# Weight sums of a seven-product feed-forward layer: 64 half-partition DMAs, one behind each block product, with two small reorderings

## The chip, the core and the metric

The kernel runs on one core of one Trainium2 chip. The metric is the device time of one launch in microseconds (us). The median of three runs before the change is 1150.55 us (1150.04 to 1153.35). One further launch was profiled; the trace that is quoted here is of that launch. The engines are called as the profile calls them: PE (TensorE matmuls) and PEld (its weight loads), DVE (VectorE), ACT (ScalarE), POOL (GpSimd), SP (SyncE, which here only issues DMAs).

## The reference

One decoder layer on 512 tokens of width 1024, in float32: a SwiGLU feed-forward half step, a token mixer (two kinds of attention), and a second feed-forward half step. "Part one" and "part two" are the two feed-forward steps. The change touches them alone:

```
def swiglu(x, w_gate, w_up, w_down):
    return (jax.nn.silu(x @ w_gate) * (x @ w_up)) @ w_down
h = rms_norm(x, ffn1_pre[l])
x = x + 0.5 * rms_norm(swiglu(h, ffn1_w_gate[l], ffn1_w_up[l], ffn1_w_down[l]), ffn1_post[l])
```

The hidden width is 2816, which is 22 blocks of 128.

## The kernel before

Every float32 matmul is made of three matmuls in a faster 32-bit format: each operand is split into a rounded part `hi` and the rest `lo`, and `hi*hi`, `hi*lo` and `lo*hi` are added up (`mm3`, L148 to L153). The rounded part of a weight tile is made by ACT (L128, tile `whi`), the rest by DVE (L129, tile `wlo`). There are three `whi` and three `wlo` buffers of 128x1024, so DVE and ACT can be at most three weight tiles ahead of PE.

Gate and up products use a scheme with seven block products in place of eight. The hidden blocks go in 11 groups p of two blocks each. Groups 0 and 1 (`PLAIN`) are computed plainly. From group 2 on, each group has seven products P1, P2, P6, P5, P7, P4, P3, with P1 of the next group between P7 and P4. A product is eight weight tiles of 128x128 against 256 token columns, 24 matmuls in all. `prep` makes its weight tile, which for P6, P5 and P3 is a sum or a difference of the four weight blocks of the group (L465: s1 = block + block; L466: s2; L480 and L477: differences made in place). `run` issues the matmuls; `finished` adds the products up: P1, P6 and P7 are copied out of PSUM by ACT into tiles `V_s` (L500), and DVE adds the next product to them (L504 behind P2, L509 behind P7, L516 behind P3). Then `swiglu` follows (L358, L359, L360), and after P3 the sums of the hidden activations (`sums`, L363 to L382), which are stored to DRAM.

Weight blocks come through a ring of three `raw` tiles of two halves each. `refill` (L314) issues the next 512 KB load on SP's queue when a half has been read for the last time. The loads stand in one list: gate and up blocks, then the blocks for the down projection.

The down projection uses the same scheme, so it needs four sums of down weights, T1 to T4. They are formed in DRAM by DMAs from DRAM to DRAM that POOL issues, some with addition (`table_sums`): for each quarter of the hidden groups, two copies, two more copies, two additions of a weight quarter, one addition of one sum to another, one more such addition. In part one this happens while the gate and up products run. The table `SUMS` says which steps follow which group: after a group's activations are there, POOL copies one column of them into a tile `mark` (L389), and the DMAs of that row of the table are issued behind this copy. In part two the sums were formed during the mixer, with the same transfers.

Part one begins in `opening`, where the order on ACT, DVE and PE is the order of the code. It computes the products of group 0 and half of group 1 on unnormalised tokens, the row of inverse norms (`row`), and the sums of tokens T1 to T4 (`scaled_sums`), which the seven products need. Elsewhere the framework's scheduler places the instructions of each engine before the launch; on the chip each engine runs its own list strictly in order.

`ffn_down` runs the products B11, T2, T3, T1, B21, B22, T4. In `product` the weights of the last `tail` hidden groups are held, so that the first 128 tokens are finished ahead of the second; B22 has tail 4, T4 has tail 6.

Of the kernel before, what the change touches and what calls it, by code (L numbers as in the profile page):

```python
# [12 lines left out]
F32 = mybir.dt.float32  # L13
# [4 lines left out]
OP = mybir.AluOpType  # L18
# [12 lines left out]
PLAIN = 2  # L31
AHEAD = 2
# [3 lines left out]
SUMS = [((0, 0),), ((0, 1), (1, 0)), ((0, 2), (1, 1)), ((0, 3), (1, 2)), ((0, 4), (2, 0)), ((1, 3), (2, 1)), ((1, 4), (2, 2)),  # L36
        ((2, 3), (3, 0)), ((2, 4), (3, 1)), ((3, 2),), ((3, 3),), ((3, 4),)]
# [24 lines left out]
class Layer:  # L62
# [257 lines left out]
    def ffn(self, gu, wd, td, post, finish, xsrc, aside=None, opened=None):  # L320
# [5 lines left out]
        later = LATER if opened else NP  # L326

# [34 lines left out]
        def sums(p, ev, od):  # L362

            h = slice(0, 256), slice(256, 512)
            x, y = self.slot("CB" if p < KEEP else "PT"), self.slot("ring")
# [17 lines left out]
        def extra(p):  # L383
            if opened:
                sums_behind((E[p] if p >= later else E[p][0].bitcast(F32))[:, 0:1], p + 1)

        def sums_behind(src, n):
            mark = self.sbt("mark", [P, 1])
            behind = nc.gpsimd.tensor_copy(mark, src).ins  # L389
            with self.tc.issue_after(behind):  # L390
                for g, step in SUMS[n]:
                    self.table_sums(wd, td, 3 * g, step)

        banks = dict(opened["banks"]) if opened else {}
        if opened:
            tops = opened["tops"]
            sums_behind(row[:, 0:1], 0)
# [97 lines left out]
        def finished(p, name):  # L495
            st = state[p]
            t0, t1 = slice(0, 256), slice(256, 512)
            if name in ("P1", "P6", "P7"):
                v = self.slot("V")
                nc.scalar.copy(v, st["X"])  # L500
                st[name + "c"] = v
            if name == "P2":
# [3 lines left out]
                st["od"] = self.slot("W")  # L506
                swiglu(st["ev"][:, t0], v[:, t0], v[:, t1], t0)
# [3 lines left out]
            elif name == "P4":  # L511
                b = st["X"]
                swiglu(st["od"][:, t0], b[:, t0], b[:, t1], t0)
            elif name == "P3":
                v = st["P6c"]
                nc.vector.tensor_add(v, st["Z"], v)  # L516
                swiglu(st["ev"][:, t1], v[:, t0], v[:, t1], t1)
# [14 lines left out]
        self.ffn_down(E, later, kept, wd, td, post, finish, xsrc, aside, opened)  # L532
# [48 lines left out]
    def scaled_sums(self, tags, xt, g, out):  # L581
# [19 lines left out]
        out["T3"] = self.keep_sum(tags, diff(4, hi, lambda j: xt[j][:, hi]))  # L601
        yield
        t1 = less(lambda j: xt[j][:, hi], lambda j: xt[j][:, lo])
        out["T1"] = self.keep_sum(tags, t1)
        yield
        t2 = diff(4, hi, of(t1))
        out["T2"] = self.keep_sum(tags, t2)
# [3 lines left out]
    def ffn_down(self, E, later, kept, wd, td, post, finish, xsrc, aside, opened):  # L611
# [91 lines left out]

        a = [self.bank("F") for _ in range(2)]
# [983 lines left out]
```

## Time and profile before

| what | value |
| --- | --- |
| median of three runs | 1150.55 us |
| the profiled launch, its own time | 1148.57 us |
| its span, from the first to the last instruction | 1146.8 us |
| mean granted TensorE clock | 0.991 |
| PE busy | 1106.8 us (97%) |
| DVE busy | 879.5 us (77%) |
| ACT busy | 638.7 us (56%) |
| POOL busy | 130.7 us (11%) |

The profiled launch took 1.77 us more than its span, the median 1.98 us more than the profiled launch. Opening and the gate and up products of part one fill the first 255 us or so; its down projection ends near 350 us. The gate and up products of part two begin near 800 us, the down projection fills the last 140 us. Times within the profile count from the first instruction. In a row of the timeline stand the start, the duration, the engine, the line, the operation and the tiles, and in brackets how long the engine had been idle and for whom. In a row of windows stand the busy time of each engine with its count of instructions, the granted clock (PEclk), the busy share of the 16 DMA engines and what they moved.

### The profile page before, as it was taken

To read this page: it belongs to the slowest core of one execution; us is meant where nothing else is said; L and a number is where in the kernel's file an instruction comes from. 1 tells how busy PE (TensorE), PEld (TensorE's weight loads), DVE (VectorE), ACT (ScalarE), POOL (GpSimd) and SP (SyncE) were. 2 spreads that over 40 slices of the span, in tenths; PEclk is the share of its full clock that TensorE was granted. 3 is DMA by queue.
4 is the path that set the end of the run, shared out by engine and by line. 5 is a ranking of instruction groups with operands and counts; after the bars stand their busy time and mean duration, and the time that the engine had idled before them with its cause. 6 is when DMAs were issued, how large, how long until landed. Compare 5 with 4: busy or idle time off the path is not lost.

```text
span 1146.8 us, 18400 instructions
## 1 busy us (share of the span) xinstructions
PE 1106.8 (97%) x6863; PEld 979.7 (85%) x6863; DVE 879.5 (77%) x1554; ACT 638.7 (56%) x1151; POOL 130.7 (11%) x186
## 2 busy tenths in 40 slices
PE   9989799999999999999999999999999999999996
PEld 7889799987878977777888898887989999998885
DVE  5978798998668788788545465885788989979574
ACT  7445345466455677687555534554435555548552
POOL 0212101100003025456000000000000000000000
PEclk9989899999999999999999999999999999999999
DMA  9879795679956369996243425475233434369862
GB/s 353 277 237 245 223 274 177 181 216 290 306 184 184 97 193 299 293 278 139 84 129 120 131 66 136 147 245 180 83 107 129 151 121 130 121 208 324 274 188 88
DMA packets 106569, 218.08 MB, mean 190 GB/s; under 512 B 20432, under 2 KB 50160, under 8 KB 106480
## 3 DMA queue, kind: packets, MB, share of 16 engines
q1 hardware_dynamic: 97120, 170.51, 45.6%
q0 software_dynamic: 9216, 46.14, 15.8%
q8 instruction: 54, 0.88, 0.3%
q10 hardware_dynamic: 144, 0.26, 0.1%
q14 instruction: 35, 0.29, 0.1%
HBM read 195.60 MB, written 67.42 MB: 229 GB/s over the span
## 4 chain that ended last, share of the span: by engine, by line
PE 59%; DVE 21%; DMA 10%; issue 4%; ACT 4%; POOL 2%; DVEq 0%; POOLq 0%; SPq 0%; ACTq 0%
PE pb_F L153 8%; PE pb_F L151 8%; PE pb_F L152 8%; DVE wlo L129 7%; PE pb_S L153 5%; PE pb_S L151 5%; PE pb_S L152 5%; DMA raw<-in_gu_dram 4%; PE pb_T L152 4%; PE pb_T L153 4%; PE pb_T L151 4%; PE pb_V L151 2%; PE pb_V L152 2%; PE pb_V L153 2%; DMA tmp_t<-in_x_dram 1%
## 5 line engine op out<-in xcount | busy, mean ns | idle before, releaser
L129 DVE TENSOR_TENSOR wlo<-raw,whi 128x1024 fp32r<-128x1024 f32 (+2 forms) x237 | 280.4, 1185 | 120.0 <-ACT whi L128 115.9
L128 ACT CAST whi<-raw 128x1024 fp32r<-128x1024 f32 (+2 forms) x237 | 241.8, 1021 | 204.6 <-PE pb_F L152 53.2
L151 PE MATMUL pb_F<-xhl_t,whi 128*128 128x512 f32 (+1 forms) x440 | 155.1, 352 | 1.7 <-DVE Q_s L1328 1.0
L153 PE MATMUL pb_F<-xhl_t,wlo 128*128 128x512 f32 (+1 forms) x440 | 154.3, 351 | 1.1 <-DVE wlo L129 1.0
L152 PE MATMUL pb_F<-xhl_t,whi 128*128 128x512 f32 (+1 forms) x440 | 153.7, 349 | 0.0
L153 PE MATMUL pb_S<-xhl_t,wlo 128*128 128x256 f32 (+1 forms) x280 | 86.0, 308 | 13.0 <-DVE wlo L129 13.0
L153 PEld LDWEIGHTS pb_F<-xhl_t,wlo 128*128 128x128 f32 x440 | 82.7, 188 | 12.0 <-DVE wlo L129 2.4
L151 PEld LDWEIGHTS pb_F<-xhl_t,whi 128*128 128x128 f32 x440 | 82.8, 188 | 11.7 <-DVE Q_s L1328 1.2
L152 PEld LDWEIGHTS pb_F<-xhl_t,whi 128*128 128x128 f32 x440 | 82.8, 188 | 9.7 <-issue 0.2
L151 PE MATMUL pb_S<-xhl_t,whi 128*128 128x256 f32 (+1 forms) x280 | 85.5, 305 | 0.1
L152 PE MATMUL pb_S<-xhl_t,whi 128*128 128x256 f32 (+1 forms) x280 | 85.1, 304 | 0.0
L172 POOL TENSOR_TENSOR rs_t<-rs_t,mhalf_t 128x1 f32<-128x1 f32 x20 | 13.0, 649 | 598.4 <-DVE rs_t L168 598.4
L153 PEld LDWEIGHTS pb_S<-xhl_t,wlo 128*128 128x128 f32 x280 | 54.7, 195 | 16.4 <-DVE wlo L129 14.2
L1077 POOL TENSOR_SCALAR SP_s<-SP_s,st_t 128x384 f32<-128x384 f32 (+2 forms) x48 | 51.7, 1129 | 71.6 <-DVE st_t L1013 61.5
L151 PEld LDWEIGHTS pb_S<-xhl_t,whi 128*128 128x128 f32 x280 | 54.6, 195 | 2.7 <-DVE V_s L509 0.3
L152 PEld LDWEIGHTS pb_S<-xhl_t,whi 128*128 128x128 f32 x280 | 54.6, 195 | 2.2
L153 PE MATMUL pb_T<-xhl_t,wlo 128*128 128x256 f32 x200 | 55.8, 279 | 0.6 <-DVE wlo L129 0.6
L151 PE MATMUL pb_T<-xhl_t,whi 128*128 128x256 f32 x200 | 55.7, 278 | 0.0
L152 PE MATMUL pb_T<-xhl_t,whi 128*128 128x256 f32 x200 | 55.5, 278 | 0.0
L465 DVE TENSOR_TENSOR tmp_t<-raw 128x1024 f32<-128x1024 f32 x18 | 22.0, 1224 | 37.8 <-DMA raw<-in_gu_dram 37.8
L151 PE MATMUL pb_S<-SP_s,whi 128*128 128x256 f32 x160 | 44.6, 279 | 1.2 <-ACT V_s L500 1.2
L128 ACT CAST whi<-tmp_t 128x1024 fp32r<-128x1024 f32 x36 | 37.8, 1051 | 12.8 <-ACT W_s L359 5.0
(837 smaller groups left out, 3236.4 us busy)
## 6 DMA issues: line engine op xcount, KB each, us to landing
raw<-in_gu_dram SPq DMA_DIRECT2D x84, 512.0 KB, 4.4
tdram<-in_d_dram POOLq DMA_DIRECT2D x36, 768.0 KB, 11.2
raw<-tdram SPq DMA_DIRECT2D x40, 512.0 KB, 4.8
raw<-in_w_in_dram SPq DMA_DIRECT2D x18, 1024.0 KB, 5.5
raw<-in_d_dram SPq DMA_DIRECT2D x30, 512.0 KB, 4.4
tdram<-tdram POOLq DMA_DIRECT2D x12, 768.0 KB, 8.7
tdram<-in_d_dram POOLq DMA_DIRECT2D x12, 512.0 KB, 9.8
odram<-W_s SPq DMA_DIRECT2D x22, 256.0 KB, 2.0
```

Of the source, the lines that this page charges most:

```text
L128: self.last_cast = self.nc.scalar.copy(dsthi, src).ins
L129: self.nc.vector.tensor_sub(dstlo, src, dsthi.bitcast(F32))
L151: mm(out, lhi, rhi, start=start, stop=False, skip_group_check=skip)
L152: mm(out, lhi, rlo, start=False, stop=False, skip_group_check=skip)
L153: mm(out, llo, rhi, start=False, stop=stop, skip_group_check=skip)
L172: nc.gpsimd.tensor_tensor(out=r, in0=v, in1=self.mhalf, op=OP.pow)
L465: nc.vector.tensor_add(s1, blk(p, 0, 1), blk(p, 1, 1))
L1077: self.last_pool = nc.gpsimd.tensor_scalar(pp, pp, st[:, 1, t:t + 1], None, op0=OP.mult).ins
```

## The change

Four things are changed.

1. The sums of part one are issued by a generator `sum_steps` in place of `table_sums`. Each transfer is cut into two of 64 partitions, so 32 become 64, in the order of `SUM_STEPS`. Two are issued behind the row of norms, two behind each plain group, and from group 2 on one behind each of six places in `finished`: behind the ACT copies of P1, P6 and P7, behind the DVE additions of P2 and P3, and at P4. The last four follow at the start of `ffn_down`. Each place has its own `mark` copy on POOL. Part two keeps `table_sums` in the mixer.
2. The sums x of the activations of groups 1 and 2 go to slots of the tag `of` in place of the one slot `CB`.
3. In `opening` the token sums are made in another order, and the squares of the tokens stand between them.
4. B22 holds three groups at its end in place of four, in both parts.

```
+SUM_STEPS = [((2, (0, 1), 0), (3, (1, 1), 0)), ((0, (1, 1), 0), (1, (1, 0), 0)), ((2, (0, 0), 1), (3, (0, 1), 1)), ((0, 2, 1),),
+             ((1, 0, 1),)]
-SUMS = [((0, 0),), ((0, 1), (1, 0)), ((0, 2), (1, 1)), ((0, 3), (1, 2)), ((0, 4), (2, 0)), ((1, 3), (2, 1)), ((1, 4), (2, 2)),
-        ((2, 3), (3, 0)), ((2, 4), (3, 1)), ((3, 2),), ((3, 3),), ((3, 4),)]
+X_TAGS = "CB", "of", "of"
...
         def sums(p, ev, od):
-            x, y = self.slot("CB" if p < KEEP else "PT"), self.slot("ring")
+            x, y = self.slot(X_TAGS[p % 3] if p < KEEP else "PT"), self.slot("ring")
...
         def extra(p):
-            if opened:
-                sums_behind((E[p] if p >= later else E[p][0].bitcast(F32))[:, 0:1], p + 1)
+            if p < PLAIN:
+                sums_behind(E[p][0][:, 0:1].bitcast(F32), 2)
 
         def sums_behind(src, n):
-            mark = self.sbt("mark", [P, 1])
-            behind = nc.gpsimd.tensor_copy(mark, src).ins
-            with self.tc.issue_after(behind):
-                for g, step in SUMS[n]:
-                    self.table_sums(wd, td, 3 * g, step)
+            if opened and n:
+                mark = self.sbt("mark", [P, 1])
+                behind = nc.gpsimd.tensor_copy(mark, src).ins
+                with self.tc.issue_after(behind):
+                    for _ in range(n):
+                        next(steps, None)
...
                 nc.scalar.copy(v, st["X"])
                 st[name + "c"] = v
+                sums_behind(v[:, 0:1], 1)
             if name == "P2":
                 v = st["P1c"]
                 nc.vector.tensor_add(v, st["Y"], v)
...
+                sums_behind(v[:, t1][:, 0:1], 1)
...
             elif name == "P4":
+                sums_behind(st["od"][:, t1][:, 0:1], 1)
...
                 nc.vector.tensor_add(v, st["Z"], v)
+                sums_behind(v[:, t1][:, 0:1], 1)
                 swiglu(st["ev"][:, t1], v[:, t0], v[:, t1], t1)
...
+        with ExitStack() as behind:
+            if opened:
+                mark = self.sbt("mark", [P, 1])
+                behind.enter_context(self.tc.issue_after(nc.gpsimd.tensor_copy(mark, E[NP - 1][:, 0:1]).ins))
+            for _ in steps:
+                pass
...
-        product(quarter, "B22", d, False, True, None, 4, None, lambda: scaled(0, 1, d[0]))
+        product(quarter, "B22", d, False, True, None, 3, None, lambda: scaled(0, 1, d[0]))
...
+    def sum_steps(self, wd, td):
+        put = self.nc.gpsimd.dma_start
+        def step(b, n):
+            q = slice(b, min(b + 3, NF // 2))
+            for i, src, add in SUM_STEPS[n]:
+                for h in (slice(0, 64), slice(64, P)):
+                    s = td[src, h, q] if isinstance(src, int) else wd[src[0], src[1], h, q]
+                    if add:
+                        put(td[i, h, q], s, accum_op=OP.add)
+                    else:
+                        put(td[i, h, q], s)
+                    yield
...
+            square(0)
+            for k in range(4):
+                nc.scalar.mul(xt[k], xt[k], gcol[:, k:k + 1])
             next(sums)
+            square(1)
+            w = self.wsplit(third[:, 0], [D])
+            self.refill(third[:, 0])
+            next(sums)
+            square(2)
+            next(sums)
+            square(3)
```

The lists of instructions show what moves. On POOL, behind the second mark of a plain group and up to the third seven-product group, there stood bursts of two to four whole transfers behind one mark (`tdram_94` is the DRAM tensor of part one's sums; 128x1536 are 128 rows of three hidden groups):

```order
L389 COPY mark_t<-Q_s 128x1 [waits Activation_49,Pool_49]
L1195 DMA tdram_94<-in_d_dram 128x1536 [waits DMASW0_49]
L1196 DMA tdram_94<-in_d_dram 128x1536 [waits DMASW1_49]
L1193 DMA tdram_94<-in_d_dram 128x1536 x2
L389 COPY mark_t<-KA_s 128x1 [waits Activation_49,Pool_49]
L1198 DMA tdram_94<-tdram_94 128x1536 [waits DMASW6_49,DMASW2_49]
L1195 DMA tdram_94<-in_d_dram 128x1536 [waits DMASW4_49,DMASW3_49]
L1196 DMA tdram_94<-in_d_dram 128x1536 [waits DMASW5_49]
```

and at the same place now, from the second plain group on:

```order
L392 COPY mark_t<-Q_s 128x1 [waits Activation_49,Pool_49]
L1215 DMA tdram_94<-in_d_dram 64x1536 x2
L392 COPY mark_t<-V_s 128x1 [waits Activation_49,Pool_49]
L1215 DMA tdram_94<-in_d_dram 64x1536
L392 COPY mark_t<-V_s 128x1 [waits DVE_49]
L1215 DMA tdram_94<-in_d_dram 64x1536
L392 COPY mark_t<-V_s 128x1 [waits Activation_49,Pool_49]
L1213 DMA tdram_94<-in_d_dram 64x1536 [waits DMASW0_49]
```

One half transfer now stands behind each mark, and a mark reads a tile `V_s` or `W_s` of the group in work, where it read finished activations.

On DVE, in the middle of a seven-product group (here the one whose s1 is made first at L465), the list stood so before:

```order
L129 TENSOR_TENSOR wlo<-raw,whi 128x1024 [waits DMAHW1_49,PE_49,Activation_49]
L369 TENSOR_TENSOR ring_s<-W_s,KB_s 128x256 [waits DVE_49]
L129 TENSOR_TENSOR KA_s<-KB_s,KA_s 128x512 [waits Activation_49]
L465 TENSOR_TENSOR tmp_t<-raw 128x1024 [waits DMAHW5_49,DMAHW3_49]
L129 TENSOR_TENSOR wlo<-raw,whi 128x1024 [waits PE_49,Activation_49]
L466 TENSOR_TENSOR tmp_t<-tmp_t,raw 128x1024 [waits DVE_49]
L480 TENSOR_TENSOR raw<-raw 128x1024
L509 TENSOR_TENSOR V_s<-pb_S,V_s 128x512 [waits Activation_49]
```

and stands so now:

```order
L130 TENSOR_TENSOR wlo<-raw,whi 128x1024 [waits DMAHW1_49,PE_49,Activation_49]
L371 TENSOR_TENSOR ring_s<-W_s,KB_s 128x256 [waits DVE_49]
L130 TENSOR_TENSOR KA_s<-KB_s,KA_s 128x512 [waits Activation_49]
L468 TENSOR_TENSOR tmp_t<-raw 128x1024 [waits DMAHW5_49,DMAHW3_49]
L130 TENSOR_TENSOR wlo<-raw,whi 128x1024 [waits PE_49,Activation_49]
L469 TENSOR_TENSOR tmp_t<-tmp_t,raw 128x1024 [waits DVE_49]
L483 TENSOR_TENSOR raw<-raw 128x1024
L514 TENSOR_TENSOR V_s<-pb_S,V_s 128x512 [waits Pool_49]
```

The order is the same; the addition behind P7 (L509, now L514) waits for POOL's mark, which itself waits for the ACT copy.

On ACT, at the end of B22 in part one (the `Q_s` and `SP_s` casts are held weights of T4, `whi` its first weights, `junk_t` squares of the output), the list stood so before:

```order
L128 CAST Q_s<-raw 128x512 [waits DMAHW7_49]
L128 CAST Q_s<-raw 128x512
L159 ACTIVATE junk_t,ss_t<-pb_S,scol_t 128x512 [waits PE_49,Activation_49]
L128 CAST whi<-raw 128x1024 [waits DMAHW3_49,DVE_49,PE_49]
L128 CAST SP_s<-raw 128x512
L128 CAST whi<-raw 128x1024 [waits DMAHW4_49,DVE_49,PE_49]
```

and stands so now:

```order
L129 CAST whi<-raw 128x1024 [waits DMAHW3_49,DVE_49,PE_49]
L129 CAST SP_s<-raw 128x512
L129 CAST Q_s<-raw 128x512 [waits DMAHW7_49]
L160 ACTIVATE junk_t,ss_t<-pb_S,scol_t 128x512 [waits PE_49,Activation_49]
L129 CAST Q_s<-raw 128x512
L129 CAST whi<-raw 128x1024 [waits DMAHW4_49,DVE_49,PE_49]
```

The cast of T4's first weights has moved ahead of the held ones and of the square.

More of the change, by code (lines that the diff above doesn't have):

```diff
@@ L326, in ffn @@
         later = LATER if opened else NP
+        steps = self.sum_steps(wd, td) if opened else iter(())
         def blk(p, h, f):
@@ L396, in ffn @@
             tops = opened["tops"]
-            sums_behind(row[:, 0:1], 0)
+            sums_behind(row[:, 0:1], 2)
         else:
@@ L531, in ffn @@
             finished(p, name)
-        self.ffn_down(E, later, kept, wd, td, post, finish, xsrc, aside, opened)
+        self.ffn_down(E, later, steps, kept, wd, td, post, finish, xsrc, aside, opened)
     def xop(self, k, c):
@@ L600, in scaled_sums @@
         of = lambda t: lambda j: t[j // 2][:, j % 2]
-        out["T3"] = self.keep_sum(tags, diff(4, hi, lambda j: xt[j][:, hi]))
+        t1 = less(lambda j: xt[j][:, hi], lambda j: xt[j][:, lo])
         yield
-        t1 = less(lambda j: xt[j][:, hi], lambda j: xt[j][:, lo])
+        t3 = diff(4, hi, lambda j: xt[j][:, hi])
+        yield
         out["T1"] = self.keep_sum(tags, t1)
+        out["T3"] = self.keep_sum(tags, t3)
         yield
         t2 = diff(4, hi, of(t1))
+        yield
         out["T2"] = self.keep_sum(tags, t2)
@@ L609, in scaled_sums, with ffn_down @@
         yield
-    def ffn_down(self, E, later, kept, wd, td, post, finish, xsrc, aside, opened):
+    def ffn_down(self, E, later, steps, kept, wd, td, post, finish, xsrc, aside, opened):
         nc = self.nc
@@ L1185, in nsa @@
             fillers()
+    def sum_steps(self, wd, td):
[9 more added lines that the diff above has]
+                        put(td[i, h, q], s)
+                    yield
+        groups = list(range(0, NF // 2, 3))
+        yield from step(0, 0)
+        for n, b in enumerate(groups):
+            yield from step(b, 1)
+            yield from step(b, 2)
+            yield from step(b, 3)
+            if n + 1 < len(groups):
+                yield from step(groups[n + 1], 0)
+            yield from step(b, 4)
     def table_sums(self, wd, td, b, step):
@@ L1585, in opening, with square @@
                         nc.tensor.matmul(banks[b], l[:, c], r, start=k == 0 and i == 0, stop=k == KT - 1 and i == 2)
-            for t in range(NT):
-                if t == 2:
-                    w = self.wsplit(third[:, 0], [D])
-                    self.refill(third[:, 0])
-                    for k in range(4):
-                        nc.scalar.mul(xt[k], xt[k], gcol[:, k:k + 1])
+            def square(t):
                 nc.scalar.activation(xn[t], xn[t], AF.Square, scale=D ** -0.5, accum_out=ss[:, t:t + 1])
```

## The prediction

> **What bounds the kernel now.** I read first the busy time by stage, then who waited for whom, then the timeline of the waiting engines, then single DMAs from issue to landing. Two stretches of part one and one of part two:
>
> ```profile
> 58.00:86.00 28.00, 23.29 (x175) 22.89 (x175) 19.66 (x26) 12.40 (x18) 3.38 (x5) 0.88 0.79 237
> 115.00:143.00 28.00, 19.98 (x158) 19.78 (x157) 19.76 (x28) 9.79 (x14) 3.73 (x4) 0.82 0.71 223
> 877.00:897.00 20.00, 20.00 (x179) 20.00 (x178) 18.21 (x24) 10.68 (x16) 0.00 (x0) 1.00 0.45 142
> ```
>
> PE never idles in part two, and DVE, second column after PEld, is busy 18.21 of 20 us. In the two stretches of part one PE idles 4.7 and 8.0 us, and the clock was granted at 0.88 and 0.82: part of the stretch ran at half clock. The waits of the first 420 us name the chain:
>
> ```profile
> DVE tmp_t L465 <- DMA raw<-in_gu_dram: 25.6, 7, 9.1
> ...
> PE pb_S L153 <- DVE wlo L129: 12.8, 4, 8.0
> ```
>
> DVE waits 25.6 us for weight loads, always at the first sum of a group (L465). It stands in DVE's strict order ahead of splits that PE needs sooner, so PE stalls behind it. PE's longest stall:
>
> ```profile
> 124.06 0.58 PE L153 MATMUL pb_S<-xhl_t,wlo 128*128 128x256 f32 x1 [8.02 <-DVE wlo L129]
> ```
>
> All eight waits of this kind, groups 3 to 10, in DVE's timeline, and below them the first and last of the same groups in part two:
>
> ```profile
> 72.56 1.22 DVE L465 TENSOR_TENSOR tmp_t<-raw 128x1024 f32<-128x1024 f32 x1 [7.27 <-DMA raw<-in_gu_dram]
> 93.25 1.23 DVE L465 TENSOR_TENSOR tmp_t<-raw 128x1024 f32<-128x1024 f32 x1 [1.44 <-DMA raw<-in_gu_dram]
> 121.64 1.22 DVE L465 TENSOR_TENSOR tmp_t<-raw 128x1024 f32<-128x1024 f32 x1 [9.15 <-DMA raw<-in_gu_dram]
> 142.41 1.23 DVE L465 TENSOR_TENSOR tmp_t<-raw 128x1024 f32<-128x1024 f32 x1 [1.53 <-DMA raw<-in_gu_dram]
> 162.16 1.23 DVE L465 TENSOR_TENSOR tmp_t<-raw 128x1024 f32<-128x1024 f32 x1 [1.11 <-DMA raw<-in_gu_dram]
> 183.73 1.23 DVE L465 TENSOR_TENSOR tmp_t<-raw 128x1024 f32<-128x1024 f32 x1 [2.93 <-DMA raw<-in_gu_dram]
> 202.89 1.22 DVE L465 TENSOR_TENSOR tmp_t<-raw 128x1024 f32<-128x1024 f32 x1
> 223.67 1.23 DVE L465 TENSOR_TENSOR tmp_t<-raw 128x1024 f32<-128x1024 f32 x1 [2.15 <-DMA raw<-in_gu_dram]
> ```
>
> ```profile
> 868.17 1.23 DVE L465 TENSOR_TENSOR tmp_t<-raw 128x1024 f32<-128x1024 f32 x1 [0.96 <-DMA raw<-in_gu_dram]
> ...
> 1004.80 1.23 DVE L465 TENSOR_TENSOR tmp_t<-raw 128x1024 f32<-128x1024 f32 x1 [1.41 <-DMA raw<-in_gu_dram]
> ```
>
> Seven groups of part one take 223.67 - 72.56 = 151.1 us. The waits inside add up to 18.3, so DVE's work is 132.8, or 18.97 a group. In part two seven groups take 136.6, or 19.52 each, PE's pace. So **DVE can wait 0.55 us a group in part one before it, and no longer PE, sets the pace**, and any wait beyond that lengthens the kernel.
>
> Why the loads are late: the L465 waits at 121.64 and 142.41 end with these two loads, whose time from issue to landing is given beneath each.
>
> ```profile
> L314 SPq DMA_DIRECT2D raw<-in_gu_dram x1: 328/328/328, 108.6 to 108.6; - x1
> DMA to landing us min/median/max: 12.9/12.9/12.9
> ```
>
> ```profile
> L314 SPq DMA_DIRECT2D raw<-in_gu_dram x1: 332/332/332, 138.8 to 138.8; - x1
> DMA to landing us min/median/max: 3.5/3.5/3.5
> ```
>
> ```profile
> 100.00:108.00 8.00, 8.00 (x73) 8.00 (x72) 7.96 (x12) 4.08 (x7) 0.00 (x0) 1.00 1.02 260
> ```
>
> The first load fell into a burst of six whole sum transfers, with the DMA engines full (1.02); the second met none.
>
> **The change, part by part.** First, **the bursts go**. The bytes stay; at most one or two half transfers are under way at once. What matters is how often the one load per group that L465 waits for meets one. On a quiet queue it lands in 3.5 us. Other landings of such loads:
>
> ```profile
> L314 SPq DMA_DIRECT2D raw<-in_gu_dram x1: 333/333/333, 179.4 to 179.4; - x1
> DMA to landing us min/median/max: 4.4/4.4/4.4
> ```
>
> ```profile
> L314 SPq DMA_DIRECT2D raw<-in_gu_dram x1: 327/327/327, 157.8 to 157.8; - x1
> DMA to landing us min/median/max: 4.3/4.3/4.3
> ```
>
> ```profile
> L314 SPq DMA_DIRECT2D raw<-in_gu_dram x1: 332/332/332, 63.8 to 63.8; - x1
> DMA to landing us min/median/max: 8.7/8.7/8.7
> ```
>
> The first two met the start of a burst and lost 0.9 and 0.8 us. With every load quiet the seven waits would be 1.44, none (9.15 less 9.4), 1.53, 0.3 (1.11 less 0.8), 2.0 (2.93 less 0.9), none and 2.15: 7.4 us. The change puts a half transfer behind nearly every product, six to a group of 19.5 us, two of them (behind P2 and P6) close to the critical load. I take a delay of 1.0 us a load, near the 0.8 and 0.9 of the two rows; the bounds are nothing and 2.5, a half transfer met in full. Of three whole transfers issued at 141 to 142 us,
>
> ```profile
> DMA to landing us min/median/max: 6.5/11.4/16.0
> ```
>
> the first, an addition, landed after 6.5 us. A load's 512 KB at the 260 GB/s of the full stretch above are 2.0 us, so 1.5 of its quiet 3.5 are start-up; 6.5 less 1.5 is 5.0, and 2.5 for half. One us adds 1.0 to the five waits that exist and some 0.75 to the two that don't, since these have a little slack: 7.4 + 6.5 = 13.9, in place of 18.3. **Gain 4.4.** The wait ahead of the seven, 7.27 with a landing of 8.7, shrinks by 8.7 - 4.5 = 4.2. **Gain 4.2.** With stalls of PE this short, the half clock goes too; it is no term of its own, since DVE set the pace in those groups.
>
> By the Trainium skill, page DMA: Bandwidth & Descriptors, section Queues, rings and completion order, a DMA engine takes turns between the queues that have work, packet by packet. By that a load would at most about double its 2.0 us of data beside any burst, landing near 5.5 us; the trace differs, with 12.9 us. By the rule the delay would be at most 2.0 us, and the worst end above some 3 us better; the forecast would stay.
>
> **The opening.** DVE makes the token sums earlier, and the three whole-block operations L465, L466 and L480 of group 2 now stand ahead of group 0's activations, in time DVE spent waiting for tokens. Two of them are new there; each step of them is
>
> ```profile
> 164.44 1.22 DVE L466 TENSOR_TENSOR tmp_t<-tmp_t,raw 128x1024 f32<-128x1024 f32 x1
> 165.58 1.22 DVE L480 TENSOR_TENSOR raw<-raw 128x1024 f32<-128x1024 f32 x1
> ```
>
> 1.14 us from start to start, so DVE enters group 2 up to 2.3 us ahead. PE's products hide the shuffle itself; without that cover a split of group 1 would come a microsecond late. I take **1.5**; bounds 0 and 2.3.
>
> **Marks.** POOL gets 46 more copies and 32 more issues. Their price:
>
> ```profile
> L389 POOL COPY mark_t<-KB_s x4: 247/672/1648, 91.3 to 158.6; 128x1 f32<-128x1 f32 x4
> ...
> L1193 POOL DMA_DIRECT2D tdram<-in_d_dram x16: 515/811/1185, 37.2 to 181.8; - x16
> ```
>
> About 1.5 us a place on an otherwise idle engine. But DVE's addition behind P7 now waits for the mark, and behind it on DVE queue the splits. The time between ACT's copy and that addition is today
>
> ```profile
> 94.93 0.57 ACT L500 COPY V_s<-pb_V 128x512 f32<-128x512 f32 x1
> ```
>
> ```profile
> 96.66 0.69 DVE L509 TENSOR_TENSOR V_s<-pb_F,V_s 128x512 f32<-128x512 f32 x1
> ```
>
> 96.66 - 95.50 = 1.2 us where it is tight. A mark of 0.67 fits; one of 1.65 costs 0.5. I take a loss of **0.5** over all groups; bounds 0 and 4 (0.5 in each).
>
> **End of B22.** PE waited here in both parts, as T4's first weights were split late:
>
> ```profile
> 345.72 0.50 PE L152 MATMUL pb_T<-wlo,V_s 128*128 128x512 f32 x1 [0.79 <-DVE wlo L129]
> ```
>
> ```profile
> 1123.94 0.51 PE L152 MATMUL pb_T<-wlo,V_s 128*128 128x512 f32 x1 [0.88 <-DVE wlo L129]
> ```
>
> ACT reached the cast only after held weights that had to land, and its buffer was still held by B22:
>
> ```profile
> 1119.61 1.14 ACT L128 CAST Q_s<-raw 128x512 fp32r<-128x512 f32 x2 [1.93 <-DMA raw<-tdram]
> ...
> 1121.23 1.04 ACT L128 CAST whi<-raw 128x1024 fp32r<-128x1024 f32 x1
> ```
>
> With tail 3 a buffer comes free a pair of hidden groups sooner and the cast goes first. **Gain 1.7**; bounds 0 and 1.7.
>
> **The last four transfers** now run in B11; two additions must land before the other two are issued, and ahead of POOL's index tables, which DVE copies at
>
> ```profile
> 262.61 0.42 DVE L844 CAST dm_s<-SP_s 128x512 f32<-128x512 int32 x1
> ```
>
> Issued near 253, one round of additions lands by about 260, so the tables come just in time: I take a loss of **0.3**, bounds 0 and 2. The other places of x (`of`) cost nothing.
>
> Sum: 4.4 + 4.2 + 1.5 - 0.5 + 1.7 - 0.3 = 11.0 us. The profiled launch took 1148.57 with a span of 1146.8, so it would take 1137.6. The median is 1.98 above that launch: **1139.5 us**.
>
> **Rivals.**
> *Full cover.* The critical loads never meet a transfer. For it: loads landed in 3.5 with the queue quiet. Against it: six transfers a group. The seven waits are 7.4 (gain 10.9), the first falls by 5.2, the opening gives 2.3, T4 1.7: 20.1 better, 1130.4.
>
> *Crowding.* Halves fill the DMA engines at every moment, so each critical load meets one whole: 7.4 + 5 x 2.5 + 2 x 2.25 = 24.4, 6.1 worse than today's 18.3; first wait 2.7 better, opening 1.5, T4 1.7, marks and tables 0.8 worse: 1.0 worse, 1151.5. A milder one, at 1.8, gives 7.4 + 9.0 + 3.1 = 19.5, 1.2 worse, first wait 3.4 better, the rest as before: 4.6 better, 1146, and is the likelier. That POOL, kept by a wait, issues two transfers together and so does not spread them as it should, gives the same. For it: the rows show a load losing 9 us beside transfers. Against it: 0.8 and 0.9 for brief meetings. The Trainium skill, same page, section Rules for kernel authors, advises against two transfers to disjoint partition halves, as they share the same engines one after the other; halving would then bring nothing by itself, and only the spacing counts. No run here shows halves yet.
>
> *Late marks, slower than before.* POOL waits for an earlier addition before it issues the next, as it did once (POOL's timeline):
>
> ```profile
> 98.04 0.81 POOL L1200 DMA_DIRECT2D tdram<-tdram  x1 [5.62 <-DMA tdram<-tdram]
> ```
>
> Then the mark of P7 is late and DVE stands. The gain of 11.0 (which holds 0.5 for marks) is eaten when DVE waits 1.4 us more in each of eight groups; at 2.0 the kernel loses 5: 1155. Against it: each addition stands four transfers or more behind what it reads, over 10 us, except at the very end.
>
> **How the numbers follow.** Forecast 0.60, full cover 0.17, crowding 0.16, late marks 0.07. The range 1130 to 1147.5 reaches from full cover to mild crowding. A measurement tells 0.3% (3.5 us) from no change, so faster means below 1147.1: the forecast, full cover and half of crowding, 0.85. The other half of crowding and little else is the same: 0.09, since its end, 1151.5, lies within 3.5 us too. Late marks slower: 0.06.
>
> **What would show it.** Right: no wait at the first sum of a group above about 3.5 us and 12 to 16 us of them in the seven groups, seven groups in 145 to 148 us, the granted clock at 1.00 from 58 to 143, no PE wait at T4's start. Crowding: such waits near 3 in each group. Late marks: DVE waiting for POOL at the addition behind P7. Wrong altogether: a long wait for a sum's landing in the down projection.

## The result, and the profile after

The changed kernel is slower. Its median is 1160.92 us (1159.77 to 1167.22, four runs), against 1150.3 us for the kernel before on the same chip (1147.17 to 1153.35, four runs). The ratio is 1.0104, with a 95% interval from 1.0058 to 1.0149. The profiled launch took 1160.49 us with a span of 1158.6, which is 11.8 us more than the span before. The prediction was 1139.5, and its range ended at 1147.5.

First the line on which the prediction rested, DVE's first sum of a group (L465 before, L468 now), in DVE's timeline of the changed kernel, groups 3 to 10:

```profile
66.38 1.23 DVE L468 TENSOR_TENSOR tmp_t<-raw 128x1024 f32<-128x1024 f32 x1 [2.35 <-DMA raw<-in_gu_dram]
91.87 1.22 DVE L468 TENSOR_TENSOR tmp_t<-raw 128x1024 f32<-128x1024 f32 x1 [6.12 <-DMA raw<-in_gu_dram]
115.96 1.23 DVE L468 TENSOR_TENSOR tmp_t<-raw 128x1024 f32<-128x1024 f32 x1 [4.85 <-DMA raw<-in_gu_dram]
139.09 1.23 DVE L468 TENSOR_TENSOR tmp_t<-raw 128x1024 f32<-128x1024 f32 x1 [3.89 <-DMA raw<-in_gu_dram]
159.45 1.23 DVE L468 TENSOR_TENSOR tmp_t<-raw 128x1024 f32<-128x1024 f32 x1 [1.72 <-DMA raw<-in_gu_dram]
181.77 1.23 DVE L468 TENSOR_TENSOR tmp_t<-raw 128x1024 f32<-128x1024 f32 x1 [3.67 <-DMA raw<-in_gu_dram]
206.86 1.23 DVE L468 TENSOR_TENSOR tmp_t<-raw 128x1024 f32<-128x1024 f32 x1 [5.85 <-DMA raw<-in_gu_dram]
229.20 1.23 DVE L468 TENSOR_TENSOR tmp_t<-raw 128x1024 f32<-128x1024 f32 x1 [3.69 <-DMA raw<-in_gu_dram]
```

The first wait fell from 7.27 to 2.35, and the one of 9.15 us is gone. But now every group waits. The last seven waits add up to 29.8 us in place of 18.3, and seven groups take 229.20 - 66.38 = 162.8 us in place of 151.1. DVE's work without them, 162.8 - 29.8 = 133.0, is what it was (132.8).

Two of the loads that end these waits (those at 206.86 and 159.45), each with its time from issue to landing:

```profile
L315 SPq DMA_DIRECT2D raw<-in_gu_dram x1: 328/328/328, 197.2 to 197.2; - x1
...
DMA to landing us min/median/max: 9.6/9.6/9.6
```

```profile
L315 SPq DMA_DIRECT2D raw<-in_gu_dram x1: 328/328/328, 154.5 to 154.5; - x1
...
DMA to landing us min/median/max: 4.9/4.9/4.9
```

And the half transfers that POOL issued in the 3 us ahead of each: first additions, with one more right behind the load, then two copies.

```profile
L1213 POOL DMA_DIRECT2D tdram<-in_d_dram x2: 765/770/774, 194.9 to 196.1; - x2
...
L1213 POOL DMA_DIRECT2D tdram<-tdram x1: 774/774/774, 198.5 to 198.5; - x1
```

```profile
L1215 POOL DMA_DIRECT2D tdram<-in_d_dram x2: 514/520/525, 152.2 to 153.5; - x2
```

The load behind two additions needed 9.6 us, the one behind two copies 4.9; on a quiet queue it was 3.5. PE then stalls behind DVE as before, at other places:

```profile
94.28 0.39 PE L154 MATMUL pb_V<-xhl_t,wlo 128*128 128x256 f32 x1 [4.02 <-DVE wlo L130]
```

```profile
209.27 0.58 PE L154 MATMUL pb_T<-xhl_t,wlo 128*128 128x256 f32 x1 [4.78 <-DVE wlo L130]
```

The windows of the prediction, for the changed kernel (busy time of PE, PEld, DVE, ACT and POOL, granted clock, busy share of the DMA engines, GB/s):

```profile
58.00:86.00 28.00, 27.14 (x237) 26.74 (x236) 24.31 (x33) 14.44 (x21) 12.25 (x19) 1.00 0.91 228
115.00:143.00 28.00, 23.95 (x188) 23.54 (x187) 23.08 (x31) 12.05 (x17) 9.71 (x15) 0.94 0.81 201
877.00:897.00 20.00, 20.00 (x179) 20.00 (x178) 17.98 (x23) 11.52 (x16) 0.00 (x0) 1.00 0.45 138
```

In these windows the clock is granted at 1.00 and 0.94 in place of 0.88 and 0.82. The low clock has moved with the stalls more than it has gone: from 58 to 143 us it is 0.96, where the prediction's sign was 1.00, and around the stall at 209.27 it is 0.69:

```profile
205.00:216.00 11.00, 6.73 (x38) 6.73 (x39) 9.14 (x10) 2.18 (x4) 1.54 (x3) 0.69 0.77 189
```

From 29 to 300 us the mean is 0.97 in both kernels. PE is busy for 23.95 of 28 us in the second window, and the waits are now spread over all groups.

Then the down projection of part one. SP's queue stood for a sum that had not landed, and behind it stood five loads of hidden blocks. The first row is from the list of SP's waits from 255 to 280 us, the others are from the timeline:

```profile
SPq L315 <- DMA tdram<-tdram: 4.9, 1, 4.9
```

```profile
269.92 0.45 DVE L860 CAST dm_s<-SP_s 128x512 f32<-128x512 int32 x1 [1.74 <-POOL SP_s L858]
...
275.41 0.62 ACT L129 CAST V_s<-SP_s 128x512 fp32r<-128x512 f32 x1 [7.62 <-DMA SP_s<-odram]
276.06 0.69 DVE L130 TENSOR_TENSOR V_s<-SP_s,V_s 128x512 fp32r<-128x512 f32 x1 [3.41 <-ACT V_s L129]
...
277.02 0.50 PE L152 MATMUL pb_S<-whi,KA_s 128*128 128x512 f32 x1 [2.54 <-ACT whi L129]
```

Matching the two traces matmul by matmul gives the account of the 11.8 us:

| place | before | after | later by |
| --- | --- | --- | --- |
| first sum of group 3 starts | 72.56 | 66.38 | -6.2 |
| first sum of group 10 starts | 223.67 | 229.20 | 5.5 |
| PE just ahead of that stall of the down projection | 264.31 | 269.70 | 5.4 |
| PE a hundred matmuls behind it | 290.13 | 298.91 | 8.8 |
| T4 under way | 349.05 | 356.44 | 7.4 |
| the 2400th matmul, in the mixer | 388.7 | 396.7 | 8.0 |
| the 4800th matmul, in part two | 835.7 | 844.9 | 9.2 |
| B22 of part two, ahead of T4 | 1117.16 | 1127.82 | 10.7 |
| last output landed | 1144.15 | 1153.37 | 9.2 |
| end of the span | 1146.8 | 1158.6 | 11.8 |

The last row is the odd one: 2.6 us are lost after the last output has landed, where the kernel does nothing more.

### The profile page after: what moved, and what is told of

Its sections match the earlier page's. It is cut to its first block, busy times and chain, and to the rows that moved or that the text cites. A ratio compares the mean times of both kernels' runs of the same rounds, so it can differ in the third digit from the quotient of the medians.

```text
span 1158.6 us, 18566 instructions
## 1 busy us (share of the span) xinstructions
PE 1111.6 (96%) x6863; PEld 985.0 (85%) x6863; DVE 882.2 (76%) x1554; ACT 639.0 (55%) x1151; POOL 175.5 (15%) x264
## 4 chain that ended last, share of the span: by engine, by line
PE 51%; DVE 20%; issue 12%; DMA 10%; ACT 3%; POOL 2%; DVEq 0%; POOLq 0%; ACTq 0%; SPq 0%
DVE wlo L130 7%; PE pb_F L154 7%; PE pb_F L152 7%; PE pb_F L153 6%; DMA raw<-in_gu_dram 6%; PE pb_S L154 4%; PE pb_S L152 4%; PE pb_S L153 4%; PE pb_T L154 3%; PE pb_T L153 3%; PE pb_T L152 3%; DMA tdram<-tdram 2%; DMA tdram<-in_d_dram 2%; PE pb_V L152 1%; PE pb_V L154 1%
## 5 line engine op out<-in xcount | busy, mean ns | idle before, releaser
L468 DVE TENSOR_TENSOR tmp_t<-raw 128x1024 f32<-128x1024 f32 x18 | 22.0, 1225 | 45.4 <-DMA raw<-in_gu_dram 45.4
L130 DVE TENSOR_TENSOR wlo<-tmp_t,whi 128x1024 fp32r<-128x1024 f32 x36 | 43.8, 1217 | 1.5 <-ACT whi L129 1.4
## 6 DMA issues: line engine op xcount, KB each, us to landing
tdram<-in_d_dram POOLq DMA_DIRECT2D x18, 768.0 KB, 10.9
```

What stands on the lines that cost most here:

```text
L130: self.nc.vector.tensor_sub(dstlo, src, dsthi.bitcast(F32))
L468: nc.vector.tensor_add(s1, blk(p, 0, 1), blk(p, 1, 1))
```

## The experiments

Times are medians, and each ratio is to the kernel before, which ran beside each of the four sets of experiments below (the first four, the next four, the next four and the last two). Its medians there were 1149.24, 1149.82, 1148.99 and 1151.86 us. "The seven" are the waits at the first sum in groups 4 to 10: 18.3 us before, 29.8 after.

### Which part of the change

Four kernels. The first undoes all but the half transfers:

```
-            x, y = self.slot(X_TAGS[p % 3] if p < KEEP else "PT"), self.slot("ring")
+            x, y = self.slot("CB" if p < KEEP else "PT"), self.slot("ring")
...
-        product(quarter, "B22", d, False, True, None, 3, None, lambda: scaled(0, 1, d[0]))
+        product(quarter, "B22", d, False, True, None, 4, None, lambda: scaled(0, 1, d[0]))
```

and the opening in its old order.

> The changed kernel with the opening, the slots of x and the tail of B22 put back as they were before: the half transfers are the only change left. Theory Q (the half transfers fall on the one load per group that DVE waits for, and the last of them come late for the down projection): the loss is all theirs, the two reorderings gave 0 to 3 us, so this takes 1160 to 1165, with about 30 us of waits at the seven first sums of a group. Rival O (the reordered opening or the shorter tail shifts buffers and costs the time): about 1150.

Measured 1161.04 us (1.0092, 1.0057 to 1.0127), the seven 29.5. The loss belongs to the half transfers. Beside them the reorderings bring nothing that the medians show (1161.04 without, 1160.92 with them). With the tail of four back, PE waits at T4 again, 0.79 and 0.43 us in the two parts.

The second puts back the table of whole transfers alone:

```
+SUMS = [((0, 0),), ((0, 1), (1, 0)), ((0, 2), (1, 1)), ((0, 3), (1, 2)), ((0, 4), (2, 0)), ((1, 3), (2, 1)), ((1, 4), (2, 2)),
+        ((2, 3), (3, 0)), ((2, 4), (3, 1)), ((3, 2),), ((3, 3),), ((3, 4),)]
...
-                sums_behind(v[:, 0:1], 1)
```

> The changed kernel with the old table of whole transfers in bursts; opening, slots of x and tail of B22 stay as changed. Theory Q: 1147 to 1150.5, the seven waits near 18 us as before, the first critical load again near 7 us. Rival O: 1158 to 1162. It also prices the reorderings: 1147 if they give the 3.2 us that the prediction put on opening and tail, 1150.5 if nothing.

Measured 1146.12 us (0.9969, 0.9950 to 0.9988), the seven 17.7, the first wait 6.46. So beside whole transfers the reorderings are worth 3.1 us by the medians; the time is 0.9 us below the expected range.

The third leaves out every sum transfer of part one, with its marks kept. Its down projection takes plain weight quarters in place of the sums, as many bytes, so its output is another:

```
-                        next(steps, None)
+                        pass
...
-        self.ring_of(gu, wd, td, (), 4)
+        self.ring_of(gu, wd, [wd[0, 1], wd[0, 0], wd[1, 0], wd[1, 1]], (), 4)
```

> The changed kernel without any sum transfer in part one: the marks stay, and the down projection of part one takes the plain weight quarters in place of the sums, so the bytes loaded there are the same and the output is another. Theory Q: the seven waits fall to about 7 us, and the down projection starts without a stall: 1128 to 1136. Rival M (the 55 marks and POOL's port cost the time): still above 1150, with the waits short but DVE or PE waiting for POOL.

Measured 1128.38 us (0.9815, 0.9771 to 0.9859). DVE's waits from 40 to 260 us:

```profile
DVE tmp_t L468 <- DMA raw<-in_gu_dram: 8.8, 6, 2.2
```

That row holds all eight; the seven are 7.6, which the prediction had put at 7.4 for a quiet queue. All 58 marks ran in this kernel, so they are not the cause. The transfers cost 1160.92 - 1128.38 = 32.5 us, their price at the end of the program (below) included.

The fourth keeps the 64 halves and only moves them within the group, away from P2 and P3:

```
-                sums_behind(v[:, 0:1], 1)
+                sums_behind(v[:, 0:1], dict(P1=2, P6=1, P7=2)[name])
...
-                sums_behind(v[:, t1][:, 0:1], 1)
+                sums_behind(v[:, t1][:, 0:1], 0)
```

> The same 64 half transfers, but none behind P2 and P3, which stand 1.6 and 5 us ahead of the critical load; in their place two behind P7 and two behind the next P1, one behind P6 and P4: still six a group. If the place within the group decides (theory Q as a matter of phase): the seven waits fall to 8 to 14 us in place of 29.8, the stall at the start of the down projection stays, 1143 to 1150. If the bytes per group decide, wherever they stand (Q as a matter of bandwidth): waits stay at 25 or more, 1157 to 1163.

Measured 1143.67 us (0.9924, 0.9897 to 0.9952). DVE's waits from 40 to 260 us, all eight groups:

```profile
DVE tmp_t L468 <- DMA raw<-in_gu_dram: 15.8, 7, 5.1
```

The seven are 13.9. The same number of transfers, the same bytes and six a group: 17 us better than the changed kernel. What decides is whether they stand ahead of the critical load. The window from 115 to 143 us shows it, here for this kernel:

```profile
115.00:143.00 28.00, 27.55 (x239) 27.22 (x238) 26.24 (x38) 14.52 (x21) 9.61 (x14) 1.00 0.89 242
```

and here for the one without sums:

```profile
115.00:143.00 28.00, 27.55 (x241) 27.24 (x240) 26.39 (x40) 14.80 (x21) 5.93 (x9) 1.00 0.34 119
```

The DMA engines are busy at 0.89 in one and 0.34 in the other, and PE loses nothing between them. Busy engines alone do no harm here. Not all of the gain stays. By the matched traces this kernel is 12.3 us ahead of the kernel before at 241 us and 7.2 at 549. It lost 3.9 of the difference in the mixer, where POOL stood for a sum of part two, and an index table that DVE needs queued behind it:

```profile
518.23 0.85 POOL L1239 DMA_DIRECT2D tdram<-tdram  x1 [3.37 <-DMA tdram<-in_d_dram]
519.39 0.63 DVE L1262 TENSOR_SCALAR W_s<-W_s 128x128 int32<-128x128 int32 x1 [4.50 <-POOL W_s L1261]
...
520.64 0.58 PE L846 MATMUL pb_S<-KA_s,Q_s 128*128 128x256 f32 x1 [4.09 <-DVE st_t L852]
```

### Which property of the transfers

The fifth turns the additions into copies at the same places:

```
-                        put(td[i, h, q], s, accum_op=OP.add)
+                        put(td[i, h, q], s)
```

> The changed kernel with every addition of part one turned into a plain copy of the same 64 rows (the sums are left out, so the output is another); places, marks and bytes written stay. Theory K (an addition keeps the DMA engines busy some twice as long as a copy, and the long landings of critical loads are those that found additions ahead of them): the seven waits fall from 29.8 to 10 to 17 us, as for the loads of groups 7 and 10, which met copies alone and landed after 4.9 and 5.0 us; 1144 to 1151. Rival (any transfer at P2 and P3 does it): waits of 24 and more, 1157 to 1163.

Measured 1148.47 us (0.9992, 0.9975 to 1.0009), the seven 18.9. The time is as expected, the waits are 1.9 above the range. Additions carry 29.8 - 18.9 = 10.9 us of the 22.2 that the transfers add to the seven.

The sixth issues the last four halves earlier:

```
-                sums_behind(v[:, 0:1], 1)
+                sums_behind(v[:, 0:1], 3 if name == "P7" and p > NP - 3 else 1)
```

> The changed kernel with two more halves behind P7 of the last two groups, so that none of the 64 is left for the start of the down projection; the order of the transfers stays. Theory L (the last sums come late, SP stands at the load of T2 and the hidden blocks queued behind that load come late): the DVE waits of 1.7 and 3.4 us and PE's stall of 2.5 us there go, 3 to 5 us better: 1156 to 1158. Rival (the queue is merely full there): the stall stays, 1160 to 1162.

Measured 1158.04 us (1.0075, 1.0053 to 1.0098), the seven 27.8. No wait of SP for a sum is left in the list of its waits there, nor DVE's for the index table. DVE still waits 2.43 us for the hidden block, and PE's 2.54 became 0.23. By the matched traces the start of the down projection costs 0.5 us against the kernel before, not 3.4. That the medians also differ by 2.9 is in part chance: the seven waits are 2.0 shorter too, and in its traced launch PE ran part two at the slower pace that the last section shows.

The seventh issues whole transfers at the better places:

```
-                for h in (slice(0, 64), slice(64, P)):
+                for h in (slice(0, P),):
...
-                sums_behind(v[:, 0:1], 1)
+                sums_behind(v[:, 0:1], dict(P1=1, P6=0, P7=1)[name])
```

> Whole transfers of 128 rows at the better places: one behind P7, the next P1 and P4 of each group, one behind the row and each plain group, the last two at the start of the down projection; 32 in all, in the same order of steps. Theory Q (the place decides, not the halving): within 3 us of the kernel with halves at these places, 1141 to 1147. Rival (the halving does some good by itself, since a half blocks the queue for less long): 1148 to 1155.

Measured 1146.14 us (0.9968, 0.9947 to 0.9989), the seven 16.2, of which 6.55 in one group that met a run of additions. Halving brings little, if anything: it is 2.5 us by the medians, and the intervals overlap.

The eighth mixes copies and additions, on the places of the fourth, and issues all 64 before the down projection:

```
-                sums_behind(E[p][0][:, 0:1].bitcast(F32), 2)
+                sums_behind(E[p][0][:, 0:1].bitcast(F32), 5)
...
+            ready = adds and not any(v[0] == adds[0][0] for v in copies)
+            add = ready and (not copies or 20 * a <= 24 * (c - 12))
+            b, i, src, h = (adds if add else copies).pop(0)
```

> Halves at the better places, two behind the row and five behind each plain group, and copies and additions in turn, as far as an addition's copies are there, in place of runs of six to eight additions; all 64 are issued before the down projection. Theories K and L together: the first sums of groups 3 to 10 wait 7 to 12 us in all, the stall at the start of the down projection goes: 1134 to 1141. If the additions have no part in it and only the end counts: 1140 to 1142. If the five copies behind the plain groups crowd the first loads: 1144 and more.

Measured 1140.53 us (0.9923, 0.9896 to 0.9950), the seven 6.0, the first 4.72, together 10.7. The time fits two of the expectations; the waits, 10.7 beside the 15.8 of the fourth kernel, speak for the mixing, though the five halves behind each plain group were changed with it.

### The price of one transfer ahead of the load

Three kernels without sums, with one kind of transfer put back. The first two have one half behind P2 in each group, a copy or an addition; the third has an addition behind P3 and one behind P2. Six half copies run ahead of the groups, behind the row and the plain groups.

```
+            for i, h in at:
+                put(td[i, h, q], wd[0, i - 2, h, q], accum_op=OP.add)
+                yield
```

> The kernel without the sums, plus one transfer per group behind P2, issued some 1.6 us ahead of the critical load: a copy of 64 rows (six copies go behind the row and the plain groups; the output is another, the other marks are left out). It measures the term that the prediction took at 1.0 us with bounds of 0 and 2.5. Theory K: a copy delays the load by 0.5 to 1.2 us, landings of 4.0 to 4.7, the seven waits near 12. Prediction's term: 4.5, waits near 14.

> The same with an addition of 64 rows in place of the copy. Theory K: 1.5 to 2.5 us of delay, landings of 5.0 to 6.0, the seven waits 17 to 24. Rival B (the long landings come from a queue that is backed up by six transfers a group; a single one ahead of the load does little): delay below 1.0, waits of 14 at most.

> An addition of 64 rows behind P3 and one behind P2, the two places ahead of the critical load, and no other. Theory K: the delays add up to 3 to 5 us, landings of 6.5 to 8.5, the seven waits 27 to 40, as in the worst groups of the changed kernel. Rival B: below 1.5 us, waits of 18 at most. If the one behind P3, which has 5 us, is done before the load comes: as with one addition.

Measured in one launch each: 1136.05, 1145.35 and 1151.01 us. Worked out from the trace, the time from issue to landing of the load that DVE waits for, groups 4 to 10:

| ahead of the load | landings, us | mean | the seven |
| --- | --- | --- | --- |
| no transfer | 3.7 3.5 3.4 3.4 3.4 3.4 3.5 | 3.5 | 7.6 |
| a half copy | 4.7 4.7 4.6 3.9 4.7 3.8 4.8 | 4.5 | 13.8 |
| a half addition | 7.0 5.4 4.9 5.1 4.9 4.9 7.1 | 5.6 | 21.8 |
| two half additions | 6.4 8.5 6.2 7.5 4.9 6.9 4.9 | 6.5 | 27.8 |
| the changed kernel | 8.1 8.6 5.8 4.9 5.1 9.6 5.0 | 6.7 | 29.8 |

A copy delays the load by 1.0 us, an addition by 2.1, two additions by 3.0. DVE's waits from 40 to 260 us, all eight groups, for one addition and for two:

```profile
DVE tmp_t L468 <- DMA raw<-in_gu_dram: 24.4, 8, 5.7
```

```profile
DVE tmp_t L468 <- DMA raw<-in_gu_dram: 30.7, 8, 4.7
```

Two additions a group, with nothing else on POOL's queue in these groups, give nearly the waits of the changed kernel (32.1 for its eight). So the rival falls by which a queue backed up by six transfers is needed: it had put the delay below 1.5. In four of the seven groups the addition behind P3 had landed before the load was issued, and there the landings are 6.4, 6.2, 4.9 and 4.9, a mean of 5.6 as with one addition. In the other three they are 8.5, 7.5 and 6.9, a mean of 7.6: a delay of 4.2, twice that of one. The other transfers of the changed kernel still add something: its four loads that met additions (groups 4, 5, 6 and 9) landed after 8.0 us on average, and the same four behind the two additions alone after 7.0. Its three that met copies landed after 5.0.

### Versions that could beat both, and the end of the program

An even turn of copies and additions, with three halves behind each plain group:

```
-            add = ready and (not copies or 20 * a <= 24 * (c - 12))
+            add = ready and (not copies or a <= c - 8)
```

> The version with copies and additions in turn, with three halves behind each plain group in place of five, strictly one copy and one addition in turn, and one more behind P7 in two later groups. If the first wait of 4.7 us there came from the five copies behind each plain group: it falls to 2 us, the eight waits to 8 to 10 us, 1137 to 1140. If not, 1140 to 1143. Both are below the kernel before and the changed one.

Measured 1143.31 us (1135.37 to 1144.7; 0.9936, 0.9909 to 0.9963). A miss: the first wait fell only to 3.61, and the eight are 14.3. So the five copies explain 1.1 us of that first wait, no more.

What was left was the end of the program. Beside POOL's last computation stands a drain instruction, which the page of the profile does not count as busy. In the changed kernel, and in the one without sums, the longest of the three drains there is the one meant (durations in ns, least, median and greatest):

```profile
L1731 POOLq DRAIN  x3: 46/102/8505, 1149.3 to 1158.4; - x3
```

```profile
L1730 POOLq DRAIN  x3: 46/102/3278, 1118.9 to 1123.8; - x3
```

Its duration in the traces:

| kernel | DMAs issued by POOL | drain, us |
| --- | --- | --- |
| no sums | 32 | 3.28 |
| one copy; one addition | 47 | 4.50 |
| two additions | 56 | 5.24 |
| before; the old table with the reorderings; whole transfers at the better places | 64 | 5.89 |
| changed; all others with 64 halves | 96 | 8.50 to 8.51 |

These lie on a line of (8.51 - 3.28)/64 = 0.082 us for each DMA. Two kernels tested it. The first has whole transfers, mixed in turn and issued in time:

```
-                for h in (slice(0, 64), slice(64, P)):
+                for h in (slice(0, P),):
...
+            add = ready and (not copies or a <= c - 5)
```

> Whole transfers again, 32 in part one: one behind P7, the next P1 and P4 of each group, one behind the row and two behind each plain group, a copy and an addition in turn, all issued before the down projection. Theory D (each transfer that POOL issues adds 0.08 us to POOL's drain behind the last output, whenever it ran): the drain is 5.9 us as with the kernel before, not 8.5, and with waits like those of the halves in turn (6 to 11 us in the seven) this takes 1136 to 1141. If whole transfers crowd the loads more, the waits are 14 to 18 and it takes 1142 to 1147.

Measured 1141.01 us (0.9910, 0.9884 to 0.9937), the drain 5.60 (0.3 below the other kernels with 64), the seven 11.1. That is at the edge of what was expected; the first wait, 5.97, is the largest left.

The second keeps the number of the transfers and takes their bytes:

```
-                    s = td[src, h, q] if isinstance(src, int) else wd[src[0], src[1], h, q]
+                    q = slice(b, b + 1)
+                    s = td[src, h, q, 0:1] if isinstance(src, int) else wd[src[0], src[1], h, q, 0:1]
```

> The 64 transfers of the changed kernel at their places, with their marks and their kinds, but each cut to one element a row (64 rows of 4 bytes); the down projection of part one takes plain weight quarters, as in the kernel without sums. It parts the number of transfers from their bytes. Theory D: POOL's drain at the end is 8.5 us against 3.3 without sums, 5.2 longer, and the waits are as without sums, some 8 us in the seven: 1132 to 1136. If neither number nor marks cost anything: 1127 to 1130. If the issues themselves hold up the critical loads: waits of 15 and more, above 1140.

Measured 1132.93 us (0.9853, 0.9818 to 0.9887), the drain 8.50. DVE's waits from 40 to 260 us, all eight groups, of which the seven are 7.6:

```profile
DVE tmp_t L468 <- DMA raw<-in_gu_dram: 9.1, 6, 2.2
```

Number and marks do nothing to the loads. The kernel takes 4.6 us more by the medians than the one without transfers. By the traces, 5.24 us lie between the landing of its last output and the end of its span, and 1.11 without transfers: 4.1 us of the difference are at the end.

Four versions with the better places (halves, halves in turn, halves strictly in turn, whole ones in turn) are 0.6 to 0.9% faster than the kernel before; the fifth, whole ones in the old order, is 0.3% faster. The intervals of the four overlap, so which of them is best stays open.

## Why the prediction was wrong

**What bounds the kernel** was right: DVE's wait for one load in each group sets the pace of part one, and with no transfer in its way the kernel takes 1149.24 - 1128.38 = 20.9 us less, near the full cover of the prediction (20.1). The closeness is in part luck: by the traces 1.5 us of it are the shorter end of the program (1.11 in place of 2.63 us behind the last output), which that sum did not hold.

**The step that failed** is "I take a delay of 1.0 us a load, near the 0.8 and 0.9 of the two rows; the bounds are nothing and 2.5, a half transfer met in full". Three things in it were wrong, and the runs separate them. The value 1.0 is the price of one half copy, and that run gave 13.8 us in the seven, where the forecast said 13.9. But half of the transfers are additions, and one costs 2.1. And the places were taken as "two of them (behind P2 and P6) close to the critical load". By the order on POOL, the one of P6 goes out 1.3 to 2.0 us behind the load and does little, while that of P3 goes out ahead of it: by 2.2 us in groups 5, 7 and 9, where it was still under way when the load was issued, and by some 5 us in the others, where it counted only if it was itself held up, as in group 4. So a load can meet two, and with two additions the mean delay is 3.0 and the worst 5.0. The bound of 2.5 fell with it: it allowed one transfer, at an addition's data time, and never two. The forecast for the seven was 13.9, they are 29.8, and this is 15.9 of the 22.9 us between the forecast of the profiled launch, 1137.6, and its 1160.49. Of the rest, 3.1 are the last four transfers, 2.6 the drain and 2.7 stay open; the small terms together came out 1.3 better than forecast.

What the two rows of 0.8 and 0.9 hid is that the old table met the load by phase. The eight landings before were 8.7, 3.5, 12.9 and then 3.3 to 4.4 us: only two met a burst in full, and in the other groups the burst was issued with the load or 1.2 to 2.0 us behind it, as the three transfers issued at 141 to 142 us, behind the load of 138.8. A burst behind the load cost it 0.9 us at most, and the run with moved halves shows again that this place is cheap. Spreading the transfers evenly removed the two bad meetings and gave every group one of 1.4 to 6.1 us.

The Trainium skill, page DMA: Bandwidth & Descriptors, section Queues, rings and completion order, has each DMA engine take turns between the queues. The trace does not bear this out as a bound on the delay: at most doubling its 2.0 us of data would land the load near 5.5 us, and it landed after 9.6 us in the changed kernel and after 8.5 us behind two additions with nothing else in POOL's queue.

**The crowding rival** named the mechanism, with a wait near 3 in each group as its sign, and they are 1.7 to 6.1. Its price, 1151.5, had the same bound of one half transfer in it, so even the rival stopped short of the measured time. The Trainium skill's advice against two transfers to partition halves (same page, section Rules for kernel authors) held: whole ones in turn, at much the same places, came out at 1141.01 (0.9910) beside 1140.53 (0.9923) for halves. The whole ones wait longer, 11.1 and 6.0 in the seven, and end sooner, with a drain of 5.60 and 8.50.

**The last four transfers**, put at 0.3 with bounds of 0 and 2, cost 3.4 us. The prediction watched the index tables, which came 1.74 us late. It missed the queue on the other side: SP issues in order, the load of T2 waited 4.9 us for the last sum, and five loads of hidden blocks queued behind it. The prediction's sign for "wrong altogether", a long wait for a sum's landing in the down projection, is this one. The run that issued the four earlier brought this down to 0.5 in its trace.

**Marks and issues.** The loss of 0.5 for the marks did not come; no addition of DVE waits for POOL, and late marks, the rival on the slower side, fell. But "about 1.5 us a place on an otherwise idle engine" left out what the issues cost at the end: 32 more DMAs make POOL's drain 2.6 us longer, all of it behind the last output.

**The small terms were right in size, as far as the traces part them.** The first wait gave 4.9 us (forecast 4.2). The opening gave 1.3 us, since group 3's sum starts 6.2 us earlier and 4.9 of them are the wait (forecast 1.5). Taken singly the new opening shows less: 1.1 us beside the old table (65.3 to 64.2 without the wait), 0.5 beside the halves (64.5 to 64.0). At T4 no row of PE waits any more, and each part gains 1.4 us there. In part one 0.8 of it is given back some 12 us later, where PE now waits for the scaled tokens:

```profile
365.65 0.55 PE L223 MATMUL pb_F<-ident_t,tmp_t 128*128 128x128 f32 x3 [1.25 <-DVE tmp_t L218]
```

That leaves 2.0 of a forecast 1.7. The half clock was no term, but it did not go as said: the second window still has 0.94, and other stalls took the place of the two.

What stays open is 2.7 us that the changed kernel loses between the end of part one's feed-forward step and the T4 of part two, where the two programs differ in little. Half of it, 1.3, falls in the mixer between 494 and 544 us; other kernels lose from nothing (copies and additions mixed) to 4.7 us (the moved halves) there by the same matching.

## What to carry to other kernels

Before spreading background transfers evenly, find the one load per round that the engine in front waits for, and count the transfers that are still under way when it is issued, each at the price of its own kind: here an addition delayed the load by 2.1 us and a copy by 1.0. Put them behind that load, where DMA engines that were busy at 0.89 cost PE nothing here, and not at an even spacing. Look for a price of each transfer at the end of the program too, and let the last ones land before a queue that issues in order has to wait for them.

## What the runs showed that was not expected

In these kernels the drain of POOL at the end of the program grows by 0.082 us for each DMA that POOL issued in the whole launch, however small and however long ago: 3.28 us with 32, 8.50 with 96, the same for 64 transfers of 256 bytes as for 64 of 384 KB. With 32 the drain ended 0.8 us before the last output had landed, with 47 0.5 us after it, with 64 1.8 and with 96 4.5 us after it: from about 40 on, each further DMA is on the path.

PE's pace has a second value at full granted clock. In part two, 877 to 897 us, the kernel before and the changed one issue 179 matmuls. The launches profiled of two versions, the one with the last halves earlier and the one with halves in turn, issued 172 and 173, at a granted clock of 1.00:

```profile
877.00:897.00 20.00, 20.00 (x172) 20.00 (x171) 18.04 (x24) 10.74 (x16) 0.00 (x0) 1.00 0.43 138
```

```profile
877.00:897.00 20.00, 20.00 (x173) 20.00 (x172) 18.23 (x24) 10.64 (x15) 0.00 (x0) 1.00 0.45 147
```

Over 150 matmuls that is 17.67 us in place of 17.00, all through part two's products. The code there is the same, so a difference of some 4 us between two profiled launches can be this alone. What sets the pace is not shown.
